# High and low activations of one product streamed in a single matmul, with the halves of the bank added by VectorE

## The chip, the core and the metric

The kernel runs on one NeuronCore of a Trainium2 chip. The metric is the device time of one execution in microseconds, the median of several runs. TensorE (PE in the profile; PEld are its weight loads) multiplies matrices into PSUM, an accumulator memory of eight banks of 512 float32 per partition. VectorE (DVE) and ScalarE (ACT) read PSUM and work element by element, GpSimd (POOL) helps with SBUF data, and SyncE (SP) issues most of the DMAs. Each engine takes its instructions in order.

## What is computed

One residual block over 512 tokens and 2048 channels. A wide input projection feeds two branches, retention (8 heads of 256) and a Mamba-2 style SSD mixer (64 heads of 64, 8 groups); each is projected back, the two are merged by sigmoid gates, and an output projection is added to the input.

```python
h = rmsnorm(x, norm1_w)
proj = h @ w_in                      # 2048 -> 22592
q, k, v, g_ret, z, xbc, dt_raw, gate_r, gate_s = split(proj)
y_r = retention(q, k, v, positions) * silu(g_ret)
y_s = rmsnorm(ssd(xbc, dt_raw, ...) * silu(z), ssd_norm_w)
p_r, p_s = y_r @ w_br_ret, y_s @ w_br_ssd      # 2048 -> 2048, 4096 -> 2048
merged = sigmoid(gate_r) * p_r + sigmoid(gate_s) * p_s
x = rmsnorm(x + merged @ w_out, norm_f_w)
```

## The kernel before

Activations are kept transposed, channels on partitions and 512 tokens along the free axis. All the large projections go through one function, `unit` (its matmuls are in `products`): 256 output columns of a weight for all 512 tokens. There are 119 units: 32 for retention, 40 in the SSD branch, 16 for the merge gates, 8 for `w_r`, 16 for the two halves of `w_s` and 7 for `w_out`; the last 256 columns of `w_out` are done apart.

**Precision.** Matmuls run in fp32r. To keep float32 accuracy each operand is split into a high part and a low part (the rest), and a product is three matmuls: high weight with high activation (L230), high weight with low activation (L231), low weight with high activation (L232). ScalarE casts the high weights (L148, tile `whi`), VectorE subtracts for the low ones (L149, tile `wlo`).

**Combined and plain units.** The contraction runs over 8 pairs `k` of 128-row blocks. In each pair the weight is a 2x2 arrangement (two rows, two column halves) and the activation too (two rows, two token halves of 256). A plain unit multiplies the four weight blocks with 512 tokens each (table `FOUR`; 512-column matmuls). A combined unit forms sums and differences of the blocks on both sides so that seven products of 256 columns do instead of eight (table `SEVEN`): VectorE makes the weight combinations (L247, L252, L253), and the activation combinations are made ahead by `first_half` and `second_half`, tile `a` (blocks 0 to 3 high, 4 to 7 the low parts of the same) and tile `b`. An entry of `SEVEN` is (bank, half of the bank, weight block, activation block):

```python
SEVEN = (((0, 0, 1, 0), (1, 0, 3, 2), (1, 1, 0, 5)),
         ((2, 0, 5, 3), (2, 1, 4, 4)),
         ((3, 0, 6, 1), (3, 1, 2, 6)))
```

So a unit uses four PSUM banks `pt[0]` to `pt[3]`. Bank 0 gets one product alone, in its first half; its second half stays unused. The other banks hold two products each. All the units of the stages up to the SSD branch, and every second one later, share the same four banks `pb0` to `pb3`; the others (`alt`) use four rotating banks named `att`, which smaller matmuls use as well.

**Order in a unit.** For the first five `k` the products go in the order of the table. For the last three (`LAST`) they go group by group, so bank 0 and 1 are complete first, then 2, then 3. The sums are then taken out of PSUM: ScalarE copies the used half of bank 0 (L290), VectorE adds bank 1 (L291), subtracts bank 2 (L292, L293) and adds bank 3 (L294), each of which builds on the one before. A bank can be written by the next unit when all its readers are done.

**What sets the order.** Each engine's order is found by the framework's scheduler from priorities and a simulated timeline. Weight preparation has a raised priority (`PRIO`), the taking-out of sums too. Weights are prefetched: `wf` has 3 buffers of two row pairs, `whi` 7 and `wlo` 6 of one pair each. A change of one instruction's length or of what it waits for can therefore reorder much of the program.

The units' results are used by small stages beside the matmuls: rotary embedding, scores and normalisation in retention; in the SSD branch a convolution (L617), transposes (L660), a decay matrix `L` that is loaded by SP (L682), turned into exponentials by ScalarE (L686, L688) and multiplied by VectorE (L689) before TensorE uses it (L693).

Of the kernel before, what the change touches and what calls it, by code (L numbers as in the profile page):

```python
# [12 lines left out]
ALU = mybir.AluOpType  # L13
# [87 lines left out]
NP = KD // 2  # L101
# [26 lines left out]
def hybrid_block(tc, A, out):  # L128
    nc = tc.nc
    PE, ACT, DVE, POOL, SP = nc.tensor, nc.scalar, nc.vector, nc.gpsimd, nc.sync  # L130
# [6 lines left out]
    op = ctx.enter_context(tc.tile_pool(name="op", bufs=2))  # L137
# [26 lines left out]
    X, R = [None] * NP, [None] * NP  # L164
# [5 lines left out]
    def high(k, x):  # L170
        return X[k][0][:, x, :] if isinstance(x, slice) or x < 4 else X[k][1][:, x - 4, :]

    def low(k, x):
        if isinstance(x, slice):
            return X[k][0][:, x.start + 4:x.stop + 4:x.step, :]
        return X[k][0][:, x + 4, :] if x < 4 else X[k][1][:, x - 1, :]

    def first_half(i, DVE=DVE, ACT=ACT):

        f, t = R[i], hp.tile([P, 8, 256], F32R, name=f"a{i}", tag=f"a{i}")  # L180
        X[i] = [t, None]
        DVE.tensor_tensor(f[:, 4, :], f[:, 0, :], f[:, 1, :], op=ALU.subtract)
        ACT.copy(t[:, 0:4, :], f[:, 1:5, :])
        yield
        DVE.tensor_tensor(t[:, 4:8, :], f[:, 1:5, :], t[:, 0:4, :].bitcast(F32), op=ALU.subtract)
        yield
# [16 lines left out]
    def pair_rows(f):  # L203
        return f[:, 0:4, :].rearrange("p (r h) t -> p r (h t)", r=2)

    def rows(src, i):
        return src[i * 256:(i + 1) * 256, :].rearrange("(r p) t -> p r t", p=P)
# [9 lines left out]
    def products(parts, pt, groups, PE=PE, after=None):  # L217


        started, ws = set(), []  # L220
        plain = groups is not SEVEN
        n = 4 if plain else 7

        def go(k, p):
            b, half, w, x = p
            hi, lo = ws[k]
            xh, xl = high(k, x), low(k, x)
            wh, wl = hi[:, w, :], lo[:, w, :]
            o = pt[b][:, half, :]
            PE.matmul(o, wh, xh, start=b not in started, stop=False, skip_group_check=True)  # L230
            PE.matmul(o, wh, xl, start=False, stop=False, skip_group_check=True)  # L231
            PE.matmul(o, wl, xh, start=False, stop=(k == NP - 1), skip_group_check=True)  # L232
            started.add(b)

        for k in range(NP):
            with tc.high_priority(offset=PRIO):
                if k % 2 == 0:
                    f2 = wp.tile([P, 2, 7, P], F32, name="wf", bufs=FB)
                    for m in range(2):
                        c = 0  # L240
                        v = pair_rows(f2[:, m])
                        for ap in parts:
                            w = ap.shape[-1]
                            SP.dma_start(out=v[:, :, c:c + w], in_=rows(ap, k + m))
                            c += w
                    if not plain:
                        first = DVE.tensor_tensor(f2[:, :, 4:6, :], f2[:, :, 1:3, :],  # L247
                                                  f2[:, :, 0:1, :].to_broadcast([P, 2, 2, P]), op=ALU.subtract)

                        if len(lows) > 2:  # L250
                            behind(first.ins, lows[-3])
                        DVE.tensor_tensor(f2[:, :, 0, :], f2[:, :, 2, :], f2[:, :, 4, :], op=ALU.add)  # L252
                        DVE.tensor_tensor(f2[:, :, 6, :], f2[:, :, 3, :], f2[:, :, 0, :], op=ALU.subtract)  # L253
                f = f2[:, k % 2]
                hi = wp.tile([P, 7, P], F32R, name="whi", bufs=HB)
                lo = wp.tile([P, 7, P], F32R, name="wlo", bufs=LB)
                part = split(hi[:, :n, :], lo[:, :n, :], f[:, :n, :])

                if 3 <= len(lows) < NP:
                    behind(part, root)  # L260
                lows.append(part.name)
            ws.append((hi, lo))
            if k < NP - LAST:
                for g in groups:
                    for p in g:
                        go(k, p)
            if after and k == 1:
                after()
        for g in groups:
            for k in range(NP - LAST, NP):  # L270
                for p in g:
                    go(k, p)

    def unit(parts, alt=False, plain=False):

        if alt:
            pt = [att_tile().rearrange("p (h t) -> p h t", h=2) for b in range(4)]
        else:
            pt = [acc.tile([P, 2, 256], F32, name=f"pb{b}") for b in range(4)]
        products(parts, pt, FOUR if plain else SEVEN)  # L280
        o = op.tile([P, 4, 256], F32, name="o")
        with tc.high_priority():
            if plain:
                for c in range(2):
                    ACT.copy(o[:, 2 * c:2 * c + 2, :], pt[2 * c][:, 0:1, :].to_broadcast([P, 2, 256]))
                    DVE.tensor_tensor(o[:, 2 * c, :], pt[2 * c][:, 1, :], o[:, 2 * c, :], op=ALU.add)
                    DVE.tensor_tensor(o[:, 2 * c:2 * c + 2, :], pt[2 * c + 1], o[:, 2 * c:2 * c + 2, :], op=ALU.add)
            else:
                p1, u = o[:, 0, :], o[:, 0:4:3, :]
                ACT.copy(p1, pt[0][:, 0, :])  # L290
                DVE.tensor_tensor(o[:, 1:3, :], pt[1], p1[:, None, :].to_broadcast([P, 2, 256]), op=ALU.add)  # L291
                DVE.tensor_tensor(u, o[:, 2:3, :].to_broadcast([P, 2, 256]), pt[2], op=ALU.subtract)  # L292
                DVE.tensor_tensor(o[:, 2, :], o[:, 0, :], pt[2][:, 1, :], op=ALU.subtract)  # L293
                DVE.tensor_tensor(u, pt[3], u, op=ALU.add)  # L294
        flat = o.rearrange("p s t -> p (s t)")
        return flat[:, 512:], flat[:, :512]
# [113 lines left out]
    for i in range(NP):  # L410
        x, y = raw[i], early[i][:, 2 * T:].rearrange("p (r t) -> p r t", r=2)
# [16 lines left out]
    for k in range(KD):  # L428
        pe.matmul(pdt[k % 2 * SH:(k % 2 + 1) * SH, :], wdt[:, k, :], raw[k // 2][:, k % 2, :],
                  start=(k < 2), stop=(k >= KD - 2))  # L430
# [76 lines left out]
    with tc.tile_pool(name="ret", bufs=1) as rp:  # L507
# [3 lines left out]
        for h in range(NH):  # L511
# [42 lines left out]
            k = rotate(KO, qk[:, 1])  # L554
            pt = []
# [17 lines left out]
            for lb in range(TB):  # L573
                ps = att_tile()
                for sb in range(lb + 1):
                    PE.matmul(ps[:, :DK], pt[sb][:, (lb - sb) * P:(lb - sb + 1) * P], v[:, sb, :],
                              start=(sb == 0), stop=(sb == lb))
# [19 lines left out]
    with tc.tile_pool(name="ssd", bufs=1) as sp:  # L597
# [30 lines left out]
        for g in range(NG):  # L628
# [14 lines left out]
            for jj in range(2):  # L643
# [5 lines left out]
                for e in range(2):  # L649
# [9 lines left out]
                    for c in range(TB):  # L659
# [4 lines left out]
                    xl = sp.tile([P, TB - 1, 2, 64], F32, name="xl")  # L664
                    POOL.tensor_tensor(xl, xd[:, :TB - 1], tail[:, :TB - 1, hs, None].to_broadcast([P, TB - 1, 2, 64]),  # L665
                                       op=ALU.mult)
                    ps = att_tile()
                    for c in range(TB - 1):
                        PE.matmul(ps[:, c * P:(c + 1) * P], Bk[:, c, :], xl[:, c].rearrange("p i d -> p (i d)"),  # L669
                                  start=True, stop=True)  # L670
# [20 lines left out]
                    for c in range(TB):  # L691
                        for i in range(2):
                            PE.matmul(pi[i * 64:(i + 1) * 64, c * P:(c + 1) * P], xd[:, c, i, :], L[:, i, c, :],  # L693
                                      start=True, stop=True)
                    pe = att_tile()
                    for c in range(1, TB):
                        PE.matmul(pe[:, c * P:(c + 1) * P], S[:, c - 1, :], Ct[:, c * P:(c + 1) * P],  # L697
                                  start=True, stop=True)
# [64 lines left out]
    with tc.tile_pool(name="fin", bufs=1) as fp:  # L763
# [24 lines left out]
        pt = [acc.tile([P, 2, 256], F32, name=f"pb{b}") for b in range(3)]  # L788
# [3 lines left out]
        o = [op.tile([P, 4, 256], F32, name="o") for h in halves]  # L792
# [77 lines left out]
```

## Time and profile before

| | |
|---|---|
| times of three runs | 2716.66, 2712.46, 2711.01 us |
| median | 2712.46 us |
| the profiled execution: span, first to last instruction | 2712.7 us |
| granted TensorE clock, mean | 0.997 |
| combined units; plain units | 108; 11 |

The page gives the profiled execution by its span; it has no separate time for it, and the span lies 0.2 us from the median. In the rows of the profile an instruction is named by engine, line, operation and output<-input tiles; tile numbers are left out, so `pb` is any of the four banks. Matmul durations contain the way through the array and overlap, so the step from one start to the next is what a matmul costs.

### The profile page before, as it was taken

What the parts mean: (1) busy time and instruction counts of PE and PEld (TensorE: products, weight loads), DVE (VectorE), ACT (ScalarE), POOL (GpSimd) and SP (SyncE); (2) the same over time, 40 slices, a digit from 0 to 9 for tenths busy, and PEclk for the clock granted to TensorE, in tenths of its full rate; (3) what the DMA queues carried; (4) which work ended last, traced back from release to release, by engine and by line L of the source; (5) the groups of instructions that cost most, each with busy time, mean ns of one, the idle gap of its engine ahead of it and who ended that gap; (6) DMA issues with size and microseconds to landing.
All of it is one profiled execution on the core that took longest, in us unless ns stands there. A gap on an engine that the chain in (4) does not pass through costs nothing.

```text
span 2712.7 us, 53151 instructions
## 1 busy us (share of the span) xinstructions
PE 2667.7 (98%) x21024; PEld 2577.0 (95%) x21024; DVE 2413.6 (89%) x3895; ACT 1345.5 (50%) x1906; POOL 186.2 (7%) x130
## 2 busy tenths in 40 slices
PE   7999999999999999999999999999999999999998
PEld 4899999999999999999999999999989989899897
DVE  8998788878879998999999998999989898899997
ACT  5434333433345656565665656565664353433543
POOL 0000000000000000000000001010000000011231
PEclk9999999999999999999999999999999999999999
DMA  5333333333333444344444434344464544567534
GB/s 159 94 98 103 93 110 101 105 94 105 106 111 111 131 126 134 105 138 124 138 131 131 131 117 134 115 136 132 131 204 151 192 160 138 179 184 234 199 123 141
DMA packets 339770, 362.54 MB, mean 134 GB/s; under 512 B 25152, under 2 KB 297792, under 8 KB 339520
## 3 DMA queue, kind: packets, MB, share of 16 engines
q1 hardware_dynamic: 321200, 325.58, 39.4%
q10 hardware_dynamic: 18320, 33.56, 3.3%
q8 instruction: 165, 2.70, 0.4%
q14 instruction: 85, 0.70, 0.1%
HBM read 321.56 MB, written 37.49 MB: 132 GB/s over the span
## 4 chain that ended last, share of the span: by engine, by line
PE 53%; DVE 3%; DMA 2%; issue 1%; ACT 1%; POOL 0%; SPq 0%; DVEq 0%; ACTq 0%; POOLq 0%
PE pb L232 14%; PE pb L231 14%; PE pb L230 14%; PE att L231 3%; PE att L232 3%; PE att L230 3%; DVE wlo L149 1%; PE pb L118 1%; PE att L693 1%; DMA L<-A_d 1%; DMA wf<-in_w_br_ssd_dram 1%; PE att L669 1%; PE att L697 1%; DMA mm_d<-f 1%; ACT L L686 0%
## 5 line engine op out<-in xcount | busy, mean ns | idle before, releaser
L148 ACT CAST whi<-wf 128x896 fp32r<-128x896 f32 (+1 forms) x968 | 832.5, 904 | 794.7 <-DVE wf L253 412.5
L149 DVE TENSOR_TENSOR wlo<-wf,whi 128x896 fp32r<-128x896 f32 (+1 forms) x968 | 1019.6, 1069 | 77.3 <-PE pb L232 49.1
L230 PE MATMUL pb<-a,whi 128*128 128x256 f32 (+1 forms) x3328 | 962.3, 294 | 7.3 <-ACT whi L148 2.7
L231 PE MATMUL pb<-a,whi 128*128 128x256 f32 (+1 forms) x3328 | 966.8, 293 | 2.7 <-DVE a L118 2.4
L232 PE MATMUL pb<-a,wlo 128*128 128x256 f32 (+1 forms) x3328 | 953.3, 292 | 5.9 <-DVE wlo L149 5.9
L230 PEld LDWEIGHTS pb<-a,whi 128*128 128x128 f32 x3328 | 636.2, 192 | 20.8 <-ACT whi L148 3.7
L230 PE MATMUL pb<-b,whi 128*128 128x256 f32 x2304 | 654.4, 284 | 0.0
L231 PEld LDWEIGHTS pb<-a,whi 128*128 128x128 f32 x3328 | 637.6, 192 | 17.3 <-DVE a L118 5.2
L231 PE MATMUL pb<-b,whi 128*128 128x256 f32 x2304 | 653.6, 284 | 0.0
L232 PE MATMUL pb<-b,wlo 128*128 128x256 f32 x2304 | 648.3, 284 | 0.0
L232 PEld LDWEIGHTS pb<-a,wlo 128*128 128x128 f32 x3328 | 629.6, 192 | 19.5 <-DVE wlo L149 8.0
L231 PEld LDWEIGHTS pb<-b,whi 128*128 128x128 f32 x2304 | 442.4, 192 | 0.0
L230 PEld LDWEIGHTS pb<-b,whi 128*128 128x128 f32 x2304 | 442.2, 192 | 0.0
L232 PEld LDWEIGHTS pb<-b,wlo 128*128 128x128 f32 x2304 | 439.8, 192 | 0.2
L247 DVE TENSOR_TENSOR wf<-wf 128x512 f32<-128x512 f32 x432 | 303.9, 703 | 52.9 <-DMA wf<-in_w_in_dram 33.8
L253 DVE TENSOR_TENSOR wf<-wf 128x256 f32<-128x256 f32 x432 | 192.2, 445 | 1.8
L252 DVE TENSOR_TENSOR wf<-wf 128x256 f32<-128x256 f32 x432 | 186.7, 432 | 0.5
L232 PE MATMUL att<-a,wlo 128*128 128x256 f32 (+1 forms) x480 | 143.9, 306 | 1.6 <-DVE wlo L149 1.6
L231 PE MATMUL att<-a,whi 128*128 128x256 f32 (+1 forms) x480 | 145.4, 305 | 0.0
L230 PE MATMUL att<-a,whi 128*128 128x256 f32 (+1 forms) x480 | 145.4, 305 | 0.0
L686 ACT ACTIVATE L<-L,sst 128x128 f32<-128x128 f32 x256 | 78.7, 389 | 58.7 <-DMA L<-A_d 58.7
L665 POOL TENSOR_TENSOR xl<-xd,sst 128x384 f32<-128x384 f32 x32 | 48.1, 1504 | 805.6 <-DVE xd L662 805.6
(218 smaller groups left out, 2776.2 us busy)
## 6 DMA issues: line engine op xcount, KB each, us to landing
wf<-in_w_in_dram SPq DMA_DIRECT2D x640, 256.0 KB, 3.0
wf<-in_w_br_ssd_dram SPq DMA_DIRECT2D x128, 256.0 KB, 3.3
wf<-in_w_out_dram SPq DMA_DIRECT2D x72, 256.0 KB, 3.3
wf<-in_w_in_dram SPq DMA_DIRECT2D x128, 128.0 KB, 2.7
L<-A_d SPq DMA_DIRECT2D x32, 512.0 KB, 4.3
wf<-in_w_br_ret_dram SPq DMA_DIRECT2D x64, 256.0 KB, 3.4
ys_d<-B ACTq DMA_DIRECT2D x32, 256.0 KB, 2.3
r<-ys_d SPq DMA_DIRECT2D x16, 512.0 KB, 5.5
```

Of the source, the lines that this page charges most:

```text
L118: ins = getattr(self.engine, name)(*args, **kw).ins
L148: ACT.copy(dst_hi, src)
L149: return DVE.tensor_tensor(dst_lo, src, dst_hi.bitcast(F32), op=ALU.subtract).ins
L230: PE.matmul(o, wh, xh, start=b not in started, stop=False, skip_group_check=True)
L231: PE.matmul(o, wh, xl, start=False, stop=False, skip_group_check=True)
L232: PE.matmul(o, wl, xh, start=False, stop=(k == NP - 1), skip_group_check=True)
L247: first = DVE.tensor_tensor(f2[:, :, 4:6, :], f2[:, :, 1:3, :], f2[:, :, 0:1, :].to_broadcast([P, 2, 2, P]), op=ALU.subtract)
L252: DVE.tensor_tensor(f2[:, :, 0, :], f2[:, :, 2, :], f2[:, :, 4, :], op=ALU.add)
L253: DVE.tensor_tensor(f2[:, :, 6, :], f2[:, :, 3, :], f2[:, :, 0, :], op=ALU.subtract)
L665: POOL.tensor_tensor(xl, xd[:, :TB - 1], tail[:, :TB - 1, hs, None].to_broadcast([P, TB - 1, 2, 64]), op=ALU.mult)
L669: PE.matmul(ps[:, c * P:(c + 1) * P], Bk[:, c, :], xl[:, c].rearrange("p i d -> p (i d)"), start=True, stop=True)
L686: ACT.activation(L[:, i, c, :], L[:, i, c, :], AF.Relu, scale=-1.0, bias=At[:, c, h0 + i:h0 + i + 1])
```

## The change

Bank 0's product in a combined unit no longer takes its three matmuls in three steps of 256 columns. The first two, which use the same high weights, become one matmul of 512 columns: the moving operand is the high block 0 and the low block 4 of tile `a`, read together by the new helper `both`, and the output is the whole bank, the high product in the first half and the low one in the second. The third matmul (low weight, high activation) still adds to the first half. When the sums are taken out, ScalarE copies the first half as before, and a new VectorE add brings in the second half.

```diff
+    def both(k, x):
+        return X[k][0][:, x:x + 5:4, :] if x < 4 else X[k][1][:, x - 4:x:3, :]
...
-            PE.matmul(o, wh, xh, start=b not in started, stop=False, skip_group_check=True)
-            PE.matmul(o, wh, xl, start=False, stop=False, skip_group_check=True)
+            if b == 0 and not plain:
+                PE.matmul(pt[0], wh, both(k, x), start=b not in started, stop=(k == NP - 1), skip_group_check=True)
+            else:
+                PE.matmul(o, wh, xh, start=b not in started, stop=False, skip_group_check=True)
+                PE.matmul(o, wh, xl, start=False, stop=False, skip_group_check=True)
             PE.matmul(o, wl, xh, start=False, stop=(k == NP - 1), skip_group_check=True)
...
                 ACT.copy(p1, pt[0][:, 0, :])
+                DVE.tensor_tensor(p1, pt[0][:, 1, :], p1, op=ALU.add)
                 DVE.tensor_tensor(o[:, 1:3, :], pt[1], p1[:, None, :].to_broadcast([P, 2, 256]), op=ALU.add)
```

In the changed kernel the wide matmul is L234, the others of a combined unit are L236 to L238 (before L230 to L232), the copy is L296, the new add L297, and the four VectorE steps behind it L298 to L301 (before L291 to L294). Lines of the SSD branch and after move by 7.

Three places show how the order changes. All are in the SSD branch. The first is TensorE at the start of a unit for `z`, in the fifth of the eight groups of heads; `pb0` and `pb1` are banks 0 and 1, `a0`, `a1`, `a2` the activation tiles of row pairs 0, 1, 2.

Before:

```order
L230 MATMUL pb0_16425<-a0_200,whi_16435 128x256
L231 MATMUL pb0_16425<-a0_200,whi_16435 128x256
L232 MATMUL pb0_16425<-a0_200,wlo_16436 128x256
L230 MATMUL pb1_16426<-a0_200,whi_16435 128x256
L231 MATMUL pb1_16426<-a0_200,whi_16435 128x256
L232 MATMUL pb1_16426<-a0_200,wlo_16436 128x256
```

Now:

```order
L234 MATMUL pb0_16019<-a0_200,whi_16029 128x512
L238 MATMUL pb0_16019<-a0_200,wlo_16030 128x256
L234 MATMUL pb0_16019<-a1_205,whi_16053 128x512
L238 MATMUL pb0_16019<-a1_205,wlo_16054 128x256
L234 MATMUL pb0_16019<-a2_211,whi_16083 128x512
L236 MATMUL pb1_16020<-a0_200,whi_16029 128x256
```

The two narrow matmuls are one wide one, and bank 0 is now served for three row pairs before the unit asks for bank 1.

The second place is VectorE where the sums of the same unit are taken out; `o` is the result, `wf` and `wlo` are weights of later row pairs, `xd` is a transposed activation of the SSD step that runs beside it.

Before:

```order
L247 TENSOR_TENSOR wf_16887<-wf_16887 128x2x256
L291 TENSOR_TENSOR o_16653<-pb1_16426,o_16653 128x512
L253 TENSOR_TENSOR wf_16831<-wf_16831 128x2x128
L252 TENSOR_TENSOR wf_16887<-wf_16887 128x2x128
L292 TENSOR_TENSOR o_16653<-o_16653,pb2_16427 128x2x256
L253 TENSOR_TENSOR wf_16887<-wf_16887 128x2x128
L293 TENSOR_TENSOR o_16653<-o_16653,pb2_16427 128x256
L149 TENSOR_TENSOR wlo_16838<-wf_16831,whi_16837 128x896
L662 TENSOR_TENSOR xd_16669<-att_16664,sst_99 128x512
L294 TENSOR_TENSOR o_16653<-pb3_16428,o_16653 128x2x256
```

Now:

```order
L253 TENSOR_TENSOR wf_16470<-wf_16470 128x2x256
L297 TENSOR_TENSOR o_16239<-pb0_16019,o_16239 128x256
L259 TENSOR_TENSOR wf_16416<-wf_16416 128x2x128
L258 TENSOR_TENSOR wf_16470<-wf_16470 128x2x128
L298 TENSOR_TENSOR o_16239<-pb1_16020,o_16239 128x512
L669 TENSOR_TENSOR xd_16256<-att_16251,sst_99 128x512
L259 TENSOR_TENSOR wf_16470<-wf_16470 128x2x128
L299 TENSOR_TENSOR o_16239<-o_16239,pb2_16021 128x2x256
L149 TENSOR_TENSOR wlo_16423<-wf_16416,whi_16422 128x896
L149 TENSOR_TENSOR wlo_16447<-wf_16416,whi_16446 128x896
L253 TENSOR_TENSOR wf_16504<-wf_16504 128x2x256
L300 TENSOR_TENSOR o_16239<-o_16239,pb2_16021 128x256
```

The new add has the place that L291 had; bank 1 comes three rows later, and the add of bank 3 (L301) follows 16 rows behind the new add, where L294 stood 8 rows behind L291.

The third place is SP's queue, where decay matrices `L`, the factors `E` and the weights `wf` are loaded, at the turn from the first group to the second.

Before:

```order
L244 DMA wf_10161<-in_w_in_dram 128x2x128 x4
L682 DMA L_9887<-A_d_89 128x1024
L244 DMA wf_10219<-in_w_in_dram 128x2x128 x4
L244 DMA wf_10277<-in_w_in_dram 128x2x128 x4
L244 DMA wf_10314<-in_w_in_dram 128x2x128 x2
L656 DMA E_9864<-E_d_90 64x384 x2
L244 DMA wf_10314<-in_w_in_dram 128x2x128 x2
L682 DMA L_10924<-A_d_89 128x1024
```

Now:

```order
L250 DMA wf_9827<-in_w_in_dram 128x2x256 x2
L689 DMA L_9649<-A_d_89 128x1024
L250 DMA wf_9916<-in_w_in_dram 128x2x128 x4
L250 DMA wf_9972<-in_w_in_dram 128x2x128 x4
L663 DMA E_9626<-E_d_90 64x384 x2
L689 DMA L_10658<-A_d_89 128x1024
L250 DMA wf_10028<-in_w_in_dram 128x2x128 x4
L250 DMA wf_10064<-in_w_in_dram 128x2x128 x4
```

The same loads are issued, but the decay matrices stand ahead of some weight loads that they stood behind.

## The prediction, made before the changed kernel was run

> **What bounds the kernel now.** I read the page's busy shares first, then busy time by stage, then what the engines wait for, and last the timeline of single matmuls.
>
> ```profile
> span 2712.7 us, 53151 instructions
> PE 2667.7 (98%) x21024; PEld 2577.0 (95%) x21024; DVE 2413.6 (89%) x3895; ACT 1345.5 (50%) x1906; POOL 186.2 (7%) x130
> ...
> core 0: us, PE busy (x) PEld busy (x) DVE busy (x) ACT busy (x) POOL busy (x), PEclk, DMA share, GB/s
> 100.00:800.00 700.00, 698.32 (x5533) 680.45 (x5533) 592.31 (x1043) 269.77 (x346) 20.65 (x32) 1.00 0.34 101
> 800.00:2000.00 1200.00, 1191.06 (x10117) 1178.42 (x10116) 1101.31 (x1747) 715.82 (x1081) 94.67 (x62) 1.00 0.43 129
> 2000.00:2190.00 190.00, 189.43 (x1324) 177.99 (x1323) 168.50 (x264) 89.65 (x119) 2.33 (x2) 1.00 0.55 181
> 2190.00:2350.00 160.00, 160.00 (x1180) 152.91 (x1179) 132.52 (x205) 67.71 (x88) 1.29 (x1) 1.00 0.51 162
> 2350.00:2540.00 190.00, 187.31 (x1296) 175.03 (x1295) 178.38 (x268) 73.48 (x98) 26.14 (x15) 1.00 0.64 203
> 2540.00:2674.00 134.00, 130.01 (x1036) 127.75 (x1035) 126.23 (x184) 69.80 (x95) 37.58 (x11) 0.99 0.40 130
> ```
>
> The stages are retention (100 to 800 us), the SSD branch with the merge gates (800 to 2000), then `w_r`, the two halves of `w_s`, and `w_out`. From 100 to 2674 us TensorE's idle time adds up to 1.7 + 8.9 + 0.6 + 0.0 + 2.7 + 4.0 = 17.9 us in 2574, at a granted clock of 1.00. VectorE, the runner-up, is busy 85% of retention, 92% of the SSD stage, 94% of the second half of `w_s` and 94% of `w_out`. So **TensorE sets the pace in every stage**, and VectorE is close behind it in the last two.
>
> TensorE's own waits, in all, number and longest, on the lines that matter here:
>
> ```profile
> PE pb L232 <- DVE wlo L149: 5.9, 7, 2.2
> PE pb L230 <- ACT whi L148: 2.7, 4, 1.0
> PE pb L230 <- DVE o L293: 1.1, 1, 1.1
> PE pb L230 <- ACT o L290: 0.5, 1, 0.5
> PE pb L230 <- DVE o L291: 0.4, 1, 0.4
> ```
>
> It waits for late weights (L149, L148) more than for a bank that is still being emptied (L290 to L293): 8.6 us against 2.0.
>
> A busy TensorE can still be made shorter, so the next question is what one matmul costs. The durations (0.28 and 0.39 us) contain the way through the array and overlap; the step from start to start is the price.
>
> ```profile
> 2054.79 0.28 PE L231 MATMUL att<-b,whi 128*128 128x256 f32 x1
> ...
> 2061.99 0.28 PE L230 MATMUL att<-b,whi 128*128 128x256 f32 x1
> ...
> 2168.31 0.28 PE L232 MATMUL pb<-b,wlo 128*128 128x256 f32 x1
> 2168.43 0.40 PE L230 MATMUL att<-a,whi 128*128 128x512 f32 x1
> ...
> 2170.50 0.39 PE L230 MATMUL att<-a,whi 128*128 128x512 f32 x1
> ...
> 2186.82 0.39 PE L230 MATMUL att<-a,whi 128*128 128x512 f32 x1
> ```
>
> From 2054.79 the last row of the first pair is 60 matmuls of 256 columns later: 7.20 / 60 = **0.1200 us each**. From 2170.50 to 2186.82 stand 72 steps of 512 columns, in a plain unit: 16.32 / 72 = **0.2267 us each**. A 256-column step takes 0.12 before a 512-column one too (2168.31 to 2168.43). 256 more columns cost 0.1067 us, so 0.0133 us of every step is paid per matmul, whatever its width.
>
> **The change, part by part.**
>
> *The matmuls.* A combined unit gives bank 0 one product in each of 8 row pairs; its first two matmuls, 256 columns each on the same high weights, become one of 512. The step goes from 2 x 0.1200 to 0.2267, **0.0133 us less**. The columns streamed stay the same; one weight load goes. The count comes from the evictions, one L291 for each combined unit:
>
> ```profile
> L291 DVE TENSOR_TENSOR o<-pb,o 128x512 f32<-128x512 f32 x96 | 66.0, 688 | 17.2 <-PE pb L232 16.1 <-ACT o L290 0.6
> L291 DVE TENSOR_TENSOR o<-att,o 128x512 f32<-128x512 f32 x12 | 8.2, 686 | 4.3 <-PE att L232 4.2
> L293 DVE TENSOR_TENSOR o<-o,pb 128x256 f32<-128x256 f32 x96 | 39.9, 415 | 0.0
> ```
>
> 96 + 12 = 108 units, times 8 is 864 pairs: 864 x 0.0133 = **11.5 us** less on the engine that bounds every stage. The two pieces that the new matmul reads (blocks 0 and 4 of tile `a`) lie apart; the plain units' products read two separate blocks as well (`A1` is blocks 0 and 3), and their steps are those 0.2267, so I charge nothing for it. Bounds for this term: 0, should the wide product cost two narrow steps, to 11.5.
>
> The Trainium skill has a rule against this term: "TensorE: Matmul & The Clock Gate", section "Back-to-back issue gap", puts a warm step at the columns over 2.4 GHz plus about 2.5 ns, so that merging two would save 2.5 ns, 2.2 us in all by an estimate from that page. The trace does not agree: its two steps leave 13.3 ns per matmul. The result by that rule is a rival below.
>
> *The new add.* Each of the 108 units gets a 128x256 VectorE add that reads PSUM, the form of L293 (0.415 us as a row). VectorE's rows overlap; its steps tell the price:
>
> ```profile
> 870.56 0.41 DVE L253 TENSOR_TENSOR wf<-wf 128x256 f32<-128x256 f32 x1
> 870.90 0.41 DVE L293 TENSOR_TENSOR o<-o,pb 128x256 f32<-128x256 f32 x1
> 871.23 0.41 DVE L252 TENSOR_TENSOR wf<-wf 128x256 f32<-128x256 f32 x1
> 871.56 0.68 DVE L294 TENSOR_TENSOR o<-pb,o 128x512 f32<-128x512 f32 x1
> ```
>
> 0.33 to 0.34 us of the queue: 108 x 0.34 = 36.7 us of VectorE. The units are 29 in retention, 55 in the SSD stage and 6 in each half of the rest, so VectorE goes to 602 of 697 us (86%), 1120 of 1194 (94%), in the second half of `w_s` 180.4 of 189.4 (95%), in `w_out` 128.3 of 133.4 (96%). None reaches 100%, so the cover is VectorE's idle time. Part of that idle time is a wait for TensorE:
>
> ```profile
> DVE wlo L149 <- PE pb L232: 49.1, 42, 2.6
> DVE o L292 <- PE pb L232: 31.6, 34, 1.4
> DVE o L291 <- PE pb L232: 16.1, 25, 2.6
> ```
>
> At 49.1 us of it VectorE had filled all six `wlo` buffers, and at 47.7 it stood ready for a bank that was still being summed. That is room for 36.7 us. If the cover were gone, all 36.7 would show; the bounds are 0 and 36.7. In the two stages where TensorE already waits for weights (2350 to 2674 us, 6.7 us idle), 12 adds make 4.1 us, and I count half, **2.0 us**. Elsewhere I count nothing for load: these two stages leave VectorE only 11.6 + 7.8 us idle, so most of the 96.8 us in which it waited for TensorE lies in the others.
>
> *The bank that is freed later.* Bank 0 was free once ScalarE had copied it; now VectorE must have added too, and L298 (once L291) and the rest stand one place later. Queued behind the add on VectorE are the weight differences and splits of the next row pairs, for which ScalarE's casts and then TensorE wait. A usual unit, from its first copy to the next unit's first matmul:
>
> ```profile
> 1441.74 0.38 ACT L290 COPY o<-pb 128x256 f32<-128x256 f32 x1 [0.60 <-PE pb L232]
> ...
> 1442.31 0.68 DVE L291 TENSOR_TENSOR o<-pb,o 128x512 f32<-128x512 f32 x1
> 1442.91 0.42 DVE L253 TENSOR_TENSOR wf<-wf 128x256 f32<-128x256 f32 x1
> ...
> 1445.85 0.36 PE L230 MATMUL pb<-a,whi 128*128 128x256 f32 x1
> ```
>
> The copy ends at 1442.12 and the bank is written again at 1445.85. An add in L291's place would end near 1442.7, 3.1 us early. The new order keeps that room: the add stands where L291 stood, and TensorE starts the next unit with bank 0 alone before it asks for bank 1. The cost is confined to places where ScalarE or VectorE lag, where 2.0 us of bank waits stand now; I add half, **1.0 us** (bounds 0 and 36.7 again, if every add came just ahead of the bank's next use).
>
> *The rest.* Two table loads fewer on ScalarE, busy 50%: nothing. No DMA is added; SP's loads change places in the SSD stage, which is a rival below, not a term.
>
> Sum: -11.5 + 2.0 + 1.0 = **-8.5 us**. The profile is of one execution with span 2712.7, 0.2 from the median 2712.46 of the runs; from the median this gives **2704.0 us**.
>
> **The rivals.**
>
> *A late copy blocks VectorE (slower).* The new add waits for ScalarE's copy in VectorE's in-order queue, ahead of weight work. ScalarE is sometimes late in the SSD stage:
>
> ```profile
> 1063.82 5.10 DMA L<-A_d
> 1069.00 2.16 ACT L L686 x7
> ```
>
> Here a decay matrix came late, seven activations followed, and a unit's copy stood behind them. VectorE has 1194 - 1120 = 74 us to spare there, 1.3 us for each of 55 units; a mean lateness past that is exposed. At 1.7 us it is 22 us: 2704.0 + 22 = 2726. For it: the add goes where it waits for the copy alone. Against it: L291 waits for this copy today, and that ended its idle time for 0.6 us in the whole kernel.
>
> *The new order costs more.* The scheduler orders the SSD stage anew, with the bank-3 add (L301) in the example 16 rows behind the first add where L294 stood 8 behind L291. If late decay matrices and late banks cost half of that stage's present 8.9 us again and some more, 5 us, the time is 2709. For it: TensorE lost those 8.9 us to just such places. Against it: 8.9 us is 0.7% of a stage in which the same work comes eight times.
>
> *The new order is luckier.* Those places may as well vanish: 5 us less, 2699.
>
> *No fixed price per matmul.* By 2.5 ns a pair, 2.2 us come off, and with 3.0 us of costs the time is 2713.3; the same goes, at 2715.5, if the change saves nothing since the wide product takes two steps. Against both: the 0.1200 and 0.2267 above.
>
> **How the numbers follow.** Forecast, 2701 to 2707: 0.60. Luckier order, about 2699: 0.12. Costlier order, about 2709: 0.17. No fixed price, 2713 to 2716: 0.04. Blocked VectorE, about 2726 and from 2718 up: 0.07. A measurement of this kernel can tell about 0.2%, 5.4 us, from no change: faster is below 2707.0 and slower above 2717.9. So faster 0.60 + 0.12 = 0.72, same 0.17 + 0.04 = 0.21, slower 0.07. The range, 2698 to 2712, takes in the forecast, the costlier order and nearly all of the luckier; about 0.15 is left out.
>
> **What the profile after would show.** The 864 wide products (L234) with steps of 0.227 us; 864 fewer matmuls and weight loads, 20160 of 21024; L297 108 times, 0.42 us as a row and no idle time before it put down to L296; VectorE's busy time up by about 37 to 45 us; its waits for TensorE at L149 shorter than 49.1 us; TensorE's idle time between 100 and 2674 us at about 21 us where it was 17.9. The prediction is wrong if the wide step is 0.240, if TensorE's waits for L149, or for L297 and L298, grow by more than 5 us, or if the decay matrices' late places multiply.

## The result and the profile after

The changed kernel takes **2778.08 us** (median of 5 runs, 2773.87 to 2780.92) against 2712.15 us for the kernel before (5 runs beside it): a ratio of 1.0237, 95% interval 1.0225 to 1.0248. It is 66 us slower. The prediction said 2704.0, in a range of 2698 to 2712. The profiled execution took 2778.08 us and its span is 2775.9, 2.2 us less; so that the span of before lay only 0.2 us from a median of times is chance, and below spans are compared with spans.

Lines of the page of the changed kernel that answer to those shown of before. First the span and the busy sums, then the wide matmuls (busy time, mean ns of one, idle time of the engine before them and what ended it). In the new code the wide matmul is L234, the narrow ones L236 to L238, the copy L296, the new add L297; SSD lines stand 7 further down (the relus of `L`, L686 before, are L693).

```profile
span 2775.9 us, 51570 instructions
PE 2690.0 (97%) x20160; PEld 2551.5 (92%) x20160; DVE 2444.6 (88%) x4003; ACT 1340.9 (48%) x1904; POOL 163.8 (6%) x130
...
L234 PE MATMUL pb<-a,whi 128*128 128x512 f32 x768 | 307.8, 407 | 33.3 <-ACT whi L148 32.0 <-DVE o L297 1.3
```

The matmuls are 20160, as the change says, so there are 864 fewer; yet the span is 63.2 us longer. The first two of the windows that were shown of before, now after (TensorE, weight loads, VectorE, ScalarE, GpSimd: busy time and count; then the granted clock of TensorE, the DMA share and GB/s):

```profile
100.00:800.00 700.00, 697.21 (x5291) 667.43 (x5290) 601.66 (x1074) 270.38 (x346) 19.76 (x32) 1.00 0.33 101
800.00:2000.00 1200.00, 1152.69 (x9186) 1115.17 (x9185) 1060.81 (x1709) 672.60 (x1024) 70.68 (x58) 0.98 0.40 120
```

Retention is as before: 2.8 us of TensorE idle where it was 1.7. In the SSD stage the idle time is 1200 - 1152.69 = 47.3 us where it was 8.9, and the clock is 0.98 where it was 1.00. By the matmuls in the trace the retention ends at 788.7 us (788.3 before) and the last matmul on a decay matrix starts at 2058.7 (1998.9 before): **59.4 of the 63.2 us between the two spans arise in the SSD stage.** Going through every step of TensorE in it, the time in gaps longer than 0.25 us (beyond what the step costs) rose from about 11.8 to 56.2 us, and the time that 256-column steps of 0.195 to 0.235 us cost over 0.12 rose from about 17.3 to 32.8: 44.4 + 15.5 = 59.9 us, all of it.

The waits, in all, number and longest, of TensorE, ScalarE and VectorE after:

```profile
PE pb L234 <- ACT whi L148: 32.0, 15, 2.7
PE pb L238 <- DVE wlo L149: 9.4, 12, 2.0
PE pb L234 <- DVE o L297: 1.3, 3, 1.0
...
ACT L L693 <- DMA L<-A_d: 140.0, 29, 7.5
...
DVE wlo L149 <- PE pb L238: 57.4, 45, 3.9
DVE o L297 <- ACT o L296: 17.7, 23, 2.2
```

TensorE hardly waits for the new add (1.3 us). It waits 15 times for cast weights, and ScalarE, which casts them, waits for decay matrices 2.4 times as long as before:

```profile
ACT L L686 <- DMA L<-A_d: 58.7, 29, 4.0
```

That is the row of before. The timeline of one such place after, ScalarE first (in brackets: idle time before, and what ended it), then SP's load of `L`, then TensorE:

```profile
1495.96 0.94 ACT L148 CAST whi<-wf 128x896 fp32r<-128x896 f32 x1
1499.41 0.38 ACT L296 COPY o<-pb 128x256 f32<-128x256 f32 x1 [2.51 <-PE pb L238]
1504.46 2.45 ACT L693 ACTIVATE L<-L,sst 128x128 f32<-128x128 f32 x8 [4.67 <-DMA L<-A_d]
...
1507.33 1.04 ACT L695 ACTIVATE L<-L 128x1024 f32<-128x1024 f32 x1
1508.28 1.76 ACT L148 CAST whi<-wf 128x896 fp32r<-128x896 f32 x2
...
1497.14 0.88 SPq L250 DMA_DIRECT2D wf<-in_w_in_dram  x2
1498.12 0.41 SPq L689 DMA_DIRECT2D L<-A_d  x1
...
1495.59 1.09 PE L700 MATMUL att<-L,xd 128*64 128x128 f32 x16
...
1506.68 0.28 PE L238 MATMUL pb<-b,wlo 128*128 128x256 f32 x1
1509.26 0.50 PE L234 MATMUL pb<-a,whi 128*128 128x512 f32 x1 [2.29 <-ACT whi L148]
```

Read it from the buffer on. `L` has one buffer; its last reader (L700) ends at 1496.7. Two weight loads stand ahead of the load of `L` in SP's queue. They wait until VectorE has freed their buffer (L149, at 1497.12), so the load of `L` is issued only at 1498.12, 1.4 us late. The matrix lands 6.3 us later, the relus start at 1504.46, the exponential follows, and the first cast behind them ends at 1509.2. From 1496.9 to 1508.3, for 11.4 us, ScalarE casts nothing; TensorE eats the stock of `whi` and stops. The same place of before, in ScalarE's timeline:

```profile
1470.73 0.94 ACT L148 CAST whi<-wf 128x896 fp32r<-128x896 f32 x1 [0.62 <-PE pb L231]
1474.24 2.46 ACT L686 ACTIVATE L<-L,sst 128x128 f32<-128x128 f32 x8 [2.56 <-DMA L<-A_d]
...
1477.69 0.92 ACT L148 CAST whi<-wf 128x896 fp32r<-128x896 f32 x1
```

There the load of `L` is issued at 1470.00, 0.1 us after the products with the old `L` end, and lands 4.2 us later; the pause without a cast is 6.0 us, and TensorE does not notice it. The same holds for the whole trace. SP's waits for the release of `L` (it stands ready at the load), before and after:

```profile
SPq L682 <- PE att L693: 52.4, 23, 5.1
...
SPq L689 <- PE att L700: 8.1, 13, 5.4
```

Head pairs come in twos. The load for the second of two follows its release by 0.04 us (the median) in both kernels. The load for the first follows it by 0.07 us before and by 2.1 us after, and takes 4.5 us to land before and 5.9 us after. From the tenth load on, `L` has one to seven fewer weight loads ahead of it than before (the order rows show one such place), and still comes late: the products that release it moved forward further. Why the transfer itself takes longer was not tested.

Of the 44 gaps over 0.25 us after in this stage, 40 fall behind the load for the *first* of two head pairs (from 1010 us on, TensorE's waits for `whi` end 8 to 12 us behind it) and 4 behind that for the second. `L` is loaded for the second of one pair at 1483.6 and for the first of the next at 1498.1, as soon as the products between are done; so ScalarE is held up twice, from 1482.2 to 1493.3 and from 1496.9 to 1508.3, with four casts between.

Then the clock drops. A window of the same columns over the next 5 us, and two matmuls from it:

```profile
1510.00:1515.00 5.00, 4.66 (x26) 4.65 (x26) 5.00 (x8) 4.72 (x7) 0.00 (x0) 0.66 0.29 95
...
1511.46 0.41 PE L236 MATMUL pb<-a,whi 128*128 128x256 f32 x1
1511.68 0.41 PE L237 MATMUL pb<-a,whi 128*128 128x256 f32 x1
```

A step takes 0.21 us instead of 0.12 for some 3.4 us, about 16 steps of 0.09 us more each: a gap of 2.3 us costs TensorE about 1.5 us more after it.

### The profile page after: what moved, and what is told of

Same layout as the page of the kernel before. It is cut to its first block, busy times and chain, and to the rows that moved or that the text cites. A ratio compares the mean times of both kernels' runs of the same rounds, so it can differ in the third digit from the quotient of the medians.

```text
span 2775.9 us, 51570 instructions
## 1 busy us (share of the span) xinstructions
PE 2690.0 (97%) x20160; PEld 2551.5 (92%) x20160; DVE 2444.6 (88%) x4003; ACT 1340.9 (48%) x1904; POOL 163.8 (6%) x130
## 4 chain that ended last, share of the span: by engine, by line
PE 74%; DVE 7%; DMA 5%; ACT 4%; issue 3%; SPq 0%; DVEq 0%; ACTq 0%; POOL 0%
PE pb L238 19%; PE pb L236 17%; PE pb L237 17%; PE pb L234 5%; PE att L238 4%; PE att L237 3%; PE att L236 3%; DMA L<-A_d 3%; DVE wlo L149 3%; ACT L L693 2%; DMA wf<-in_w_in_dram 2%; PE att L583 1%; PE att L568 1%; DVE wf L253 1%; PE pb L118 1%
## 5 line engine op out<-in xcount | busy, mean ns | idle before, releaser
L149 DVE TENSOR_TENSOR wlo<-wf,whi 128x896 fp32r<-128x896 f32 (+1 forms) x968 | 1010.5, 1062 | 88.9 <-PE pb L238 57.4
L238 PE MATMUL pb<-a,wlo 128*128 128x256 f32 (+1 forms) x3328 | 928.3, 295 | 9.4 <-DVE wlo L149 9.4
L236 PE MATMUL pb<-a,whi 128*128 128x256 f32 (+1 forms) x2560 | 749.9, 298 | 6.8 <-DVE o L298 2.0
L237 PE MATMUL pb<-a,whi 128*128 128x256 f32 (+1 forms) x2560 | 750.7, 297 | 3.7 <-DVE a L118 2.5
L236 PE MATMUL pb<-b,whi 128*128 128x256 f32 x2304 | 659.3, 286 | 0.0
L238 PE MATMUL pb<-b,wlo 128*128 128x256 f32 x2304 | 651.6, 285 | 0.0
L238 PEld LDWEIGHTS pb<-a,wlo 128*128 128x128 f32 x3328 | 614.8, 192 | 25.5 <-DVE wlo L149 12.4
L236 PEld LDWEIGHTS pb<-a,whi 128*128 128x128 f32 x2560 | 489.5, 191 | 37.5 <-issue 3.7
L237 PEld LDWEIGHTS pb<-a,whi 128*128 128x128 f32 x2560 | 489.3, 191 | 31.5 <-DVE a L118 5.2
L236 PEld LDWEIGHTS pb<-b,whi 128*128 128x128 f32 x2304 | 442.2, 192 | 1.1 <-issue 1.0
L238 PEld LDWEIGHTS pb<-b,wlo 128*128 128x128 f32 x2304 | 440.5, 192 | 1.4 <-issue 1.2
L253 DVE TENSOR_TENSOR wf<-wf 128x512 f32<-128x512 f32 x432 | 303.7, 703 | 61.9 <-DMA wf<-in_w_in_dram 47.9
L234 PE MATMUL pb<-a,whi 128*128 128x512 f32 x768 | 307.8, 407 | 33.3 <-ACT whi L148 32.0
L259 DVE TENSOR_TENSOR wf<-wf 128x256 f32<-128x256 f32 x432 | 185.7, 430 | 1.8
L258 DVE TENSOR_TENSOR wf<-wf 128x256 f32<-128x256 f32 x432 | 186.6, 432 | 0.2
L234 PEld LDWEIGHTS pb<-a,whi 128*128 128x128 f32 x768 | 146.8, 191 | 41.8 <-ACT whi L148 35.1
L693 ACT ACTIVATE L<-L,sst 128x128 f32<-128x128 f32 x256 | 78.5, 389 | 155.8 <-DMA L<-A_d 140.0
L238 PE MATMUL att<-a,wlo 128*128 128x256 f32 (+1 forms) x480 | 143.1, 305 | 2.1 <-DVE wlo L149 2.1
L237 PE MATMUL att<-a,whi 128*128 128x256 f32 (+1 forms) x384 | 118.5, 311 | 0.0
```

The lines of the kernel that those rows point to most:

```text
L149: return DVE.tensor_tensor(dst_lo, src, dst_hi.bitcast(F32), op=ALU.subtract).ins
L234: PE.matmul(pt[0], wh, both(k, x), start=b not in started, stop=(k == NP - 1), skip_group_check=True)
L693: ACT.activation(L[:, i, c, :], L[:, i, c, :], AF.Relu, scale=-1.0, bias=At[:, c, h0 + i:h0 + i + 1])
```

## The experiments

Two theories stood against each other. **Order**: the new instructions cost little, and the order in which all engines issue the SSD stage costs 60 us. **Work**: the wide matmul or the add costs it. Several kernels below hold an order fixed by this:

```diff
         hybrid_block(tc, aps, out)
+        in_the_order(nc, tc)
```

where the new function makes each instruction wait, within its engine's queue alone, for the one that a written list names before it. Ratios are to the kernel before on the same chip, with 95% intervals. The kernel before was not run held to its own order; the eighth kernel, held in the same way to that order, has a ratio of 0.9989, so holding an order costs nothing near 60 us.

### The change in the order of before

All engines keep before's order; a wide matmul stands at the first of the two that it replaces, an add just ahead of its L298.

> The changed kernel, with every engine held to the order of the kernel before (the wide matmul in the place of the first of the two it replaces, the add just ahead of L298). Order theory (the new order of issue causes the loss): 2703 to 2716 us, no TensorE wait for L148 above 6 us in all. Load theory (36.7 us more work on VectorE, and the add that waits for ScalarE's copy, cause it): the work is still there, so 2755 us or more.

2719.4 us, ratio 1.0026 (1.0016 to 1.0035). The 66 us shrink to 7. Most of what is left is one wait:

```profile
PE pb L234 <- DVE o L297: 5.6, 2, 4.0
```

ScalarE's and VectorE's timelines there:

```profile
122.25 0.36 ACT L296 COPY o<-pb 128x256 f32<-128x256 f32 x1
...
123.04 2.10 DVE L149 TENSOR_TENSOR wlo<-wf,whi 128x896 fp32r<-128x896 f32 x2
125.05 0.70 DVE L253 TENSOR_TENSOR wf<-wf 128x512 f32<-128x512 f32 x1
125.65 0.43 DVE L297 TENSOR_TENSOR o<-pb,o 128x256 f32<-128x256 f32 x1
```

The copy is done at 122.6, the add starts at 125.65, behind other work in VectorE's queue, and TensorE waits 4.05 us for bank 0.

### The kernel before in the order of the change

No wide matmul, no add; only the order.

> The kernel before, narrow matmuls and no add, with every engine held to the order of the changed kernel. Order theory: 2765 to 2785 us, slow in the SSD stage alone. Load theory: no extra work, so 2708 to 2720 us.

2780.45 us, ratio 1.0258 (1.0241 to 1.0274). The old work in the new order is as slow as the change, with the same waits:

```profile
PE pb L230 <- ACT whi L148: 29.3, 15, 3.3
...
ACT L L686 <- DMA L<-A_d: 132.9, 28, 6.9
```

This settles between the two theories: it is the order.

### The change with only SP in the order of before

> The changed kernel in its own order on all engines but SP, which issues its loads in the order of the kernel before. If the late decay matrices (loads that stand behind weight loads in SP's queue, 2 to 4 us after their buffer is free) are what makes the new order slow: the load follows its free buffer by under 1 us, TensorE's 32.0 us of waits for L148 fall below 15, and the time is 2710 to 2745 us. If the order on ScalarE, VectorE and TensorE is what counts: 2765 to 2780 us.

2898.86 us, ratio 1.069 (1.0674 to 1.0706). The expectation failed, by its sign. SP's old order has the loads of `L` behind up to eight more weight loads than the new order has, while ScalarE and TensorE ask for them at the new, earlier places:

```profile
PE pb L234 <- ACT whi L148: 50.8, 15, 6.5
...
ACT L L693 <- DMA L<-A_d: 190.0, 26, 18.0
```

So the orders of the engines belong together. That the later loads of `L` are what costs more is read from these waits; this kernel also moves every other load.

### The change outside the SSD stage

A flag, false while the SSD stage is written, takes the old branch there, and leaves the add out; 53 of 108 combined units are changed, and the scheduler is free.

```diff
-            if b == 0 and not plain:
+            if b == 0 and not plain and wide[0]:
```

> The change in the 53 combined units outside the SSD stage only; the scheduler chooses the order. Both theories place the loss in the SSD stage, so about 2712 us: 53 x 8 = 424 wide matmuls at 5 ns less each are 2.1 us off, and 1 to 4 us come back as waits. Above 2725 us the loss isn't bound to the SSD stage.

2709.13 us, ratio 0.9993 (0.9984 to 1.0003): no loss, and no gain that can be told. The loss needs the SSD stage.

### Loads of `L` two weight loads earlier, in the order of the change

From the tenth on, the load for each second head pair (12 loads) is moved up by one weight tile on SP:

```diff
+SP  L689 DMA L<-A_d
 SP  L250 DMA wf<-in_w_in_dram x2
-SP  L689 DMA L<-A_d
```

> The changed kernel in its own order, but from the tenth decay matrix on every second one is loaded one weight tile (two loads) earlier in SP's queue; all else stays. If late decay matrices cost the time: they follow their free buffer about 1 us earlier than the present 1.7 to 4.6, and the time falls to 2740 to 2768 us. If lateness isn't the cause, or only the order on the other engines: 2772 to 2782 us.

2807.9 us, ratio 1.0353 (1.0338 to 1.0369): 30 us slower than the change, where I expected a gain. The wait changed places:

```profile
SPq L689 <- PE att L700: 91.0, 16, 7.8
...
DVE wf L253 <- DMA wf<-in_w_in_dram: 109.7, 60, 6.9
...
PE pb L236 <- DVE o L300: 43.2, 19, 4.3
PE pb L234 <- ACT whi L148: 18.1, 14, 3.0
```

The moved load stands in SP's queue before its buffer is free (91.0 us of waiting); the weights behind it come late (VectorE waits 109.7 us for them, 47.9 in the change); the emptying of bank 2 (L300) stands behind that on VectorE, and TensorE waits 43.2 us for the bank. TensorE's wait for `whi` did fall, from 32.0 to 18.1, but the loads that I moved were the second head pairs', which were on time (0.04 us after the release), and the gaps of the change stand behind the first ones', which come late. So this kernel does not test the theory that it was made for. No run moves the first pairs' loads alone. What it shows is that a place ahead of the release hands the wait to the loads behind. The kernel before waits so too (52.4 us) and loses nothing; here the weights behind were wanted at once.

### Loads of `L` later, in the order of before

The kernel before in its own order, with the loads for 11 second head pairs later on SP:

```diff
-SP  L682 DMA L<-A_d
 SP  L244 DMA wf<-in_w_in_dram x2
+SP  L682 DMA L<-A_d
```

> The kernel before in its own order, but from the tenth decay matrix on every second one (11 of them) is loaded two weight loads later in SP's queue; nothing else is changed. If late decay matrices cost the time: they now follow their free buffer by 2 to 7 us where it was 0.3, and the time rises by 20 us or more, to above 2732. If lateness isn't the cause: 2708 to 2720 us.

2765.29 us, ratio 1.0189 (1.0175 to 1.0202). Eleven late loads are enough to cost 51 us with nothing else changed:

```profile
PE att L693 <- DVE L L689: 36.8, 11, 6.0
...
ACT L L686 <- DMA L<-A_d: 110.3, 27, 10.9
```

Here TensorE waits at the product with `L` itself, eleven times, and hardly for `whi` (3.4 us). So it shows that late loads of `L` can cost this much, but by another wait than the change's.

### The add alone, and the wide matmul alone, in the order of before

The add alone keeps two narrow matmuls, now into the two halves of the bank:

```diff
-                PE.matmul(pt[0], wh, both(k, x), start=b not in started, stop=(k == NP - 1), skip_group_check=True)
+                PE.matmul(pt[0][:, 0, :], wh, xh, start=b not in started, stop=False, skip_group_check=True)
+                PE.matmul(pt[0][:, 1, :], wh, xl, start=False, stop=(k == NP - 1), skip_group_check=True)
```

> Two narrow matmuls as before, but the second into bank 0's other half, and the new add on VectorE; every engine in the order of the kernel before. It has the price of the add without the gain: 2716 to 2724 us (5 us of it the wait for bank 0 at about 126 us, where the add stands behind 14 other VectorE instructions). If the add is hidden, 2710 to 2715.

2721.27 us, ratio 1.0031 (1.0019 to 1.0043): the 108 adds cost 8 us (5 to 12), among it one wait of 4.0 us for the chain behind an add (`PE pb L234 <- DVE o L298`), as in the first experiment.

The wide matmul alone drops the line of the add, so it leaves out the second half of bank 0 (high weights with low activations of the first product):

> The wide matmul without the add, every engine in the order of the kernel before; the bank's second half, the product of high weights with low activations, is left out of the result. It has the gain without the price. At 0.2267 us a wide step: 11.5 us less, 2698 to 2703. At the 0.235 us that the changed kernel showed: 4.3 us less, 2705 to 2710.

2710.23 us, ratio 0.9989 (0.998 to 0.9997): a gain of 3 us (1 to 5), not 11.5.

### The order of the change without every second load of `L`

`few` is a tile of two values a partition, `tri` a constant.

```diff
+                    if e:
+                        SP.dma_start(out=few, in_=A_d[hs, :1].partition_broadcast(P))
+                    else:
...
-                            ACT.activation(L[:, i, c, :], L[:, i, c, :], AF.Relu, scale=-1.0,
+                            ACT.activation(L[:, i, c, :], tri if e else L[:, i, c, :], AF.Relu, scale=-1.0,
```

> The changed kernel in its own order of issue on every engine, but the second head pair of each two (16 of 32) no longer loads L: its relus read a constant tile of the same shape in place of the loaded one, and a load of 8 bytes a partition stands at the load's place on SP. This leaves out the decay rows of these 16 head pairs, so their share of the SSD is not the reference's. Theory (the second head pair's L chain is what comes late in the new order; casts queued behind its relus make TensorE wait): those relus no longer wait 4 to 5 us for a transfer, ScalarE's wait for the L transfer falls from 140.0 us to below 75, TensorE's wait for whi on ScalarE from 32.0 us to below 10, and the time is 2712 to 2732. Rival (the new order costs by its evictions and the 108 adds, wherever L stands): the time stays at 2760 to 2780.

2721.99 us, ratio 1.004 (1.0025 to 1.0055). With 16 transfers out of the way, all in the same order, 11 of the 66 us over before are left. Its waits, and its SSD window (all lines of this kernel's SSD stage stand 4 further down):

```profile
PE pb L234 <- ACT whi L148: 4.9, 9, 1.0
...
ACT L L697 <- DMA L<-A_d: 32.6, 13, 3.7
```

```profile
800.00:2000.00 1200.00, 1183.09 (x9614) 1146.80 (x9613) 1110.75 (x1785) 710.60 (x1071) 73.42 (x61) 1.00 0.40 119
```

The copies and adds are all still there, so the rival is out: what costs in the new order hangs on the loads of `L`. The way in which it helps is not quite the one expected. The gaps of the change stand behind the *first* head pair's load, which this kernel still makes; but with the second head pair's relus started early, ScalarE reaches that wait earlier and with more casts done, and from 1000 us on the waits that were 1.6 to 2.9 us are below 1.2, with the clock at 1.00. The first pairs' loads also come 0.9 us after their release (the median) where it was 2.1. That this is how the one load helps the next is read from the timelines, not tested by itself; the kernel also moves 8 MB less.

### The change in the order of before, adds moved up

Each add stands right behind the end of its copy in the first experiment's profile; at 126 us:

```diff
+DVE L297 TENSOR_TENSOR o<-pb,o
 DVE L149 TENSOR_TENSOR wlo<-wf,whi x2
 DVE L253 TENSOR_TENSOR wf<-wf
-DVE L297 TENSOR_TENSOR o<-pb,o
```

> The change in the order of issue of before, as in the first experiment, but on VectorE each add is moved up to just behind the end of its copy (where the profile of the first experiment shows VectorE free to take it). Theory (the adds themselves are covered; what was lost there is the one add that stood behind other VectorE work at 126 us, 4.05 us of TensorE's time, with a rest of about 3 us from other late adds): 2708 to 2715, ratio 0.998 to 1.001. Rival (36 us more of VectorE work delays TensorE wherever the adds stand): 2717 to 2722, as in the first experiment.

2715.9 us, ratio 1.0015 (1.0004 to 1.0026), just past the theory's 2715 and short of the rival's 2717; its interval overlaps that of the first experiment. The wait for the add is no longer among the five largest of TensorE, but the gain of moving the adds is not resolved, and none on before is left. In its profile TensorE idles longer than before in the second half of `w_s` and in `w_out`:

```profile
2347.00:2540.00 193.00, 187.15 (x1241) 172.65 (x1240) 179.01 (x273) 73.56 (x97) 26.50 (x15) 0.99 0.63 199
2540.00:2677.00 137.00, 130.97 (x993) 125.83 (x992) 129.12 (x190) 69.59 (x96) 23.34 (x11) 0.99 0.39 127
```

5.9 + 6.0 = 11.9 us, where before had 2.7 + 4.0 = 6.7.

### Each part alone, in the order that it gets by itself

The kernels of the seventh and eighth experiment without a fixed order:

> The add without the wide matmul (two narrow matmuls into the two halves), in the order that the scheduler gives this kernel by itself. In that order the L matmuls of the two head pairs stand 10.4 and 11.2 us of TensorE streaming apart (at 0.12 us per 256 columns), as in the changed kernel (10.4 and 10.8); in before it is 10.6 and 14.3. Theory (the add's place in the program is enough to give the costly order): 2770 to 2790. Rival (the wide matmul, or both together, give it): below 2730.

> The wide matmul without the add, in the order that the scheduler gives this kernel by itself; leaves out the second half of the bank (high weights by low activations of the first product). In that order the L matmuls of the two head pairs stand 12.5 and 13.0 us of TensorE streaming apart. Theory (a distance above about 12 us covers the L chain of about 10 us and the load's lateness): 2704 to 2716. Rival (any new order costs, about 60 us): 2750 or more.

The add alone: 2774.74 us, ratio 1.0234 (1.022 to 1.0248). The wide matmul alone: 2709.59 us, ratio 0.9993 (0.9983 to 1.0002). ScalarE's and TensorE's rows, the add alone first:

```profile
PE pb L234 <- ACT whi L148: 22.3, 9, 3.4
...
ACT L L694 <- DMA L<-A_d: 137.3, 26, 8.2
```

```profile
PE pb L234 <- ACT whi L148: 4.4, 3, 2.1
...
ACT L L692 <- DMA L<-A_d: 104.6, 31, 4.9
```

Both came as expected. The add is enough to make the scheduler choose a costly order. It is near the change's, not the same: TensorE waits less for `whi` there, and more at other places. The wide matmul alone also gets a new order, in which ScalarE waits 104.6 us for `L` (140.0 in the change) and the first pairs' loads are about as late, 1.9 us after their release; but TensorE's two products with `L` stand further apart there (1442.7 to 1457.5 in its trace, 14.8 us, and 15.3 in the next pair; the change has 13.1 and 12.8), two casts stand between the second head pair's relus and its exponential, where the change has none, and TensorE waits only 4.4 us. Which of the two spares it was not separated; it can't be the distance alone, as before has 16.6 and 13.0, the second no longer than the change's. ScalarE's waiting is not itself the loss; the loss is what stands behind it when too little is in stock.

## Why the prediction was wrong

**The step that failed** is the one under "The rest": "SP's loads change places in the SSD stage, which is a rival below, not a term". The rival was priced at 5 us, from the 8.9 us that TensorE idled there before, with "8.9 us is 0.7% of a stage in which the same work comes eight times" against it. But that idle time was the result of an order with room in it, not a price for any order, and the repetition worked the other way: one bad place, a wait for `whi`, came behind 15 of the 16 pairs of head pairs. The change in its own order against the change in the old one puts the term at 2778.08 - 2719.4 = 59 us (58 if each is first taken against the kernel before on its own chip); the old work loses 69 us by the new order. What could have been read beforehand: the order rows show the load of `L` ahead of weight loads that it stood behind, which looks like a gain, and only the place of the products that release it tells whether it is one. In the trace of before, the release of `L`, its transfer (4.3 us at the median), eight relus (2.46) and the exponential (1.06) give the pause without a cast, to be held against the stock of `whi`. I did not work out that chain for the new places.

**The wide product**, 0.0133 us less each, 11.5 us in all: mis-sized. The runs give 3 us (1 to 5). A wide step behind a narrow one, two rows from the timeline of after:

```profile
1504.68 0.39 PE L234 MATMUL pb<-a,whi 128*128 128x512 f32 x1
1504.91 0.28 PE L238 MATMUL pb<-a,wlo 128*128 128x256 f32 x1
```

0.23 us (0.235 is the median over the trace, where wide steps in a row are 0.227), so a pair saves 2 x 0.120 - 0.235 = 0.005 us, 4.3 us for 864. The prediction took its step from plain units, where all steps are wide, and called the fixed part the same for every step. A row that could have raised the doubt was among those quoted: 2168.43 is a wide matmul behind a narrow one, and its own step, in the trace of before, is 0.233 us. The bound given (0 to 11.5) held. The rival "no fixed price per matmul" had the better size.

The Trainium skill's "TensorE: Matmul & The Clock Gate", section "Back-to-back issue gap", adds about 2.5 ns per matmul to the time of its columns, so 2.2 us by an estimate from it. The saving of the wide matmul alone agrees with it within its interval (1 to 5 us), where the prediction set it aside. The steps themselves do not: by an estimate from that section of the Trainium skill, which gives its gap for a matmul by itself, they would be 0.109 and 0.216 us for 256 and 512 columns, and the trace has 0.120 and 0.235.

**The add**, 2.0 us, and **the bank freed later**, 1.0 us: together the add alone shows 8 us (5 to 12). The bounds held, the size was too small. About half is one late add at 126 us (a wait of 4.0 us), which is the "every add came just ahead of the bank's next use" case at a single place; the profile with adds moved up has 5 us more of idle time in the two stages that the prediction had named. Sum of the measured parts: -3 + 8 = +5 us, and the change in the old order measures +7 (4 to 9). So even with the order as it was, the forecast's sign was wrong.

**A late copy blocks VectorE** (the rival that ended slower): `DVE o L297 <- ACT o L296` does come, 17.7 us in 23 waits, where I said none would. It is not what costs: with the adds moved up it is 24.9 us in 27 waits, and the time is 0.15% over before.

**What was to be seen.** The count of matmuls came as said, the waits for L149 (57.4 us) did not get shorter than 49.1, VectorE is 31 us busier (37 to 45 were said), TensorE's idle time between 100 and 2674 us is 58.6 us (about 21 was said), and the last condition that would make the prediction wrong, "if the decay matrices' late places multiply", is what happened.

## What to carry to other kernels

Where a scheduler makes the order, price the new order as a term: take the single-buffered loads, and for each new place follow the chain from the release of the buffer over the queue of the engine that issues, the transfer and the work on the engine that waits, up to what stands behind it in that engine's queue. Then run the old work in the new order and the new work in the old one; the two runs separate order from work at once. A load placed ahead of its buffer's release hands the wait to what is queued behind it: harmless where that can wait, costly where it can't.

## What the hardware showed that was not expected

TensorE's clock fell after pauses of about 2 us. After the wait of 2.29 us at 1509.26 the granted clock was 0.66 over the next 5 us; after a wait of 1.7 us that ended at 1418.06 it stayed at 1.00, and after one of 2.7 us that ended at 1835.71 it was 0.50:

```profile
1406.00:1421.00 15.00, 12.56 (x97) 11.88 (x97) 12.93 (x24) 7.72 (x16) 1.27 (x1) 1.00 0.42 119
1421.00:1426.00 5.00, 5.00 (x43) 4.95 (x43) 5.00 (x6) 4.55 (x7) 1.94 (x1) 1.00 0.67 199
...
1836.00:1841.00 5.00, 5.00 (x23) 4.78 (x23) 5.00 (x8) 4.72 (x7) 0.00 (x0) 0.50 0.27 94
```

It is not a sharp bound: after a wait of 1.4 us at 1088.91 slow steps came too. The Trainium skill's "TensorE: Matmul & The Clock Gate", section "What's actually happening", has half the clock after an idle window of about 3.4 us. The half clock agrees: 0.50 in the window from 1836, and the slow step of 0.21 us is twice the 0.107 us that the prediction gives to 256 columns. The pause that led to it here was shorter: no wait of TensorE in the SSD stage was longer than 2.7 us.
